# Layer 0's up projection: two more plain features, the token sums spread by a table, jobs in a queue, sums fetched ahead

## Chip, cores and metric

The kernel runs on one core of one Trainium2 chip. The metric is the device time of one execution in microseconds (us); the profile shows one execution, instruction by instruction. The engines are TensorE (PE; its weight loads are listed as PEld), VectorE (DVE), ScalarE (ACT), GpSimd (POOL) and SyncE (SP), which issues most transfers.

## The reference, cut to what matters

One sequence of 512 tokens, 1024 channels, two layers. The change lies in layer 0's gated MLP, with 2816 hidden features:

```python
def conv_glu_ffn(h, w_in, conv_w, conv_b, w_out):
    u = h @ w_in                                  # "up": 1024 -> 2 x 2816
    c = causal_depthwise_conv(u, conv_w, width=3) + conv_b
    a, g = c[..., :D_FF], c[..., D_FF:]
    return (a * jax.nn.silu(g)) @ w_out           # "down": 2816 -> 1024

hn = rms_norm(h, norm_ffn[i])
h = h + conv_glu_ffn(hn, ffn_w_in[i], ffn_conv_w[i], ffn_conv_b[i], ffn_w_out[i])
```

## The kernel before, in words

Activations lie with the channels on the 128 partitions and the 512 tokens along the row, in 8 tiles `h`. Every product is made of three matmuls (`mm3`, L85 to L89): weight and activation are split in a high part, which ScalarE rounds (L101, L402, L426), and a low part, the remainder, which VectorE or GpSimd subtracts (L104, L403, L427). The three are high x high, high x low, low x high.

Layer 0's MLP is `mlp_halves` (L359). A hidden *feature* j is 128 value columns and 128 gate columns, 22 in all.

- *Plain features* (`PLAIN` = 5, j = 0 to 4) are two *chunks* each, gate then value (`todo`, L483). A chunk multiplies 8 weight blocks by 512 tokens: 24 matmuls, 512 wide. Its weights (`load`, L487) come by SP into one of three `raw` buffers, and GpSimd does the low part, 256 columns at a time. The chunk runs on the unnormed input; the norm's statistics (`norm.stats`, at half of chunk 2, L508) and their spread over the partitions (`norm.spread`, in chunk 3, L510) come meanwhile, and `late` (L383) multiplies the finished chunk in its bank by `rb`, then convolves it, applies silu to the gate (`gated`) or multiplies by the gate and splits (`valued`, which appends to the list `z`).
- *Features by sums* (j = 5 to 21) halve tokens and channels and make seven products of half the width in place of eight: with sums of token halves (tiles `th`, `tl`, built once for all features by `first_part` and `second_part`, L405 and L415, mostly on VectorE) and sums of weight blocks R, U, W, Q (`half_weights`, L430). U is fetched by SP and completed by a transfer issued from GpSimd that adds on landing (L441); GpSimd then makes W of R and U (L444, L445). A product is 4 blocks of 3 matmuls, 256 wide: 12; a feature has 84. Between products ScalarE copies parts out (`s1`, `s2`, `s3`, tag `sn`) and VectorE puts the result together (L562, L567, L568), then `gated` and `valued` run directly.
- *Down* is a stream of units: `down(g)` (L455) takes a group of features of `z` (`DOWN0` = 3, 5, 5, 5, 4) and goes over the 8 output tiles m; a unit is one `mm3`, 512 wide, 176 in all. Its weights go through the `raw` buffers too, one step (one m) ahead. `fill` (L533) puts units between the products of a feature, 6 per feature for j = 6 to 9, and 10 for j = 10 to 21; 32 units are left after the loop. When the last group has finished tile m, `after0` splits it for the attention and adds its square to the next norm (L210 to L213, tag `sq`, two buffers).

All parts and late chunks come out in one place in the code: in chunk 3, first all four first parts, the first late chunk, all four second parts (L513 to L517), and from then on each pending chunk at the end of a plain chunk. The first `half_weights` stands in the last plain chunk (L506), each further one at the start of the feature before its use.

The engines work off their own queues in order. The builder may bring an independent instruction forward in its queue; `pin` keeps the order of the code. PSUM has 8 banks: `rings` hands them out in turn, 6 to up (`ps`), and 6 and 7 to the norm and down (`aux`); the attention's first product uses 6 and 7 as well.

Of the kernel before, what the change touches and what calls it, by code (L numbers as in the profile page):

```python
# [26 lines left out]
P = 128  # L27
D = 1024
S = 512
# [31 lines left out]
def trunk(ctx: ExitStack, tc: tile.TileContext, x_tok, x_t, vecs, w_pool, w_kq, w_v, w_o, gain, w_in, w_half, w_down, w_end, w_tok, out):  # L61
# [288 lines left out]
    def conv_sum(fp, ps, m, name):  # L350

        cw = [col(V_CW + t * 2 * NF + m) for t in range(3)]
        t = fp.tile([P, S], F32, tag="t", name=f"{name}_t", bufs=4)
        A.activation(t, ps, AF.Identity, bias=col(V_CB + m), scale=cw[2])
        V.scalar_tensor_tensor(t[:, 1:], ps[:, : S - 1], cw[1], t[:, 1:], ALU.mult, ALU.add)  # L355
        V.scalar_tensor_tensor(t[:, 2:], ps[:, : S - 2], cw[0], t[:, 2:], ALU.mult, ALU.add)  # L356
        return t

    def mlp_halves(fp, xs, norm, ws0, after):  # L359

        lo, hi = slice(0, HS), slice(HS, S)
        z, gate = [], {}
        th, tl, ys = [], [], []

        def gated(j, ps):
            gate[j] = conv_sum(fp, ps, NF + j, f"g{j}")
# [2 lines left out]
        def valued(j, ps):  # L369
            t = conv_sum(fp, ps, j, f"a{j}")  # L370
            V.tensor_tensor(t, t, gate.pop(j), ALU.mult)
            own = j % 10 < 2
            zh, zl = (
                fp.tile([P, S], F32R, tag=f"z{k}", name=f"z{j}{k}", bufs=2)
                if own
                else xp.tile([P, S], F32R, tag=f"x{k}", name=f"z{j}{k}")
                for k in "hl"
            )
            A.activation(zh, t, AF.Copy)
            V.tensor_tensor(zl, t, zh.bitcast(F32), ALU.subtract)  # L380
            z.append((zh, zl))
# [5 lines left out]
        def spare(i, name):  # L387
            return fp.tile([P, 1024], F32R, tag="vh" if i % 6 < 3 else "vl", name=name, bufs=3)
# [26 lines left out]
        def second_part(p):  # L415
            y = ys[p]
            v = spare(p + 4, f"tv{p}").bitcast(F32).rearrange("p (a b) -> p a b", a=4)
            V.tensor_tensor(v[:, 0, :], y[:, 3, :], y[:, 2, :], ALU.add)
            V.tensor_tensor(v[:, 1, :], y[:, 3, :], y[:, 0, :], ALU.add)
            V.scalar_tensor_tensor(v[:, 2, :], y[:, 2, :], -1.0, v[:, 1, :], ALU.mult, ALU.subtract)  # L420
            V.tensor_tensor(v[:, 3, :], y[:, 1, :], v[:, 2, :], ALU.subtract)
            split_part(v, p, 3, 7)

        def own_split(raw, name):
            x, y = (fp.tile([P, 1024], F32R, tag=f"v{k}", name=f"{name}_{k}", bufs=3) for k in "hl")
            A.activation(x, raw, AF.Copy)  # L426
            V.tensor_tensor(y, raw, x.bitcast(F32), ALU.subtract)  # L427
            return x, y

        def half_weights(j):  # L430

            src = w_half[j - PLAIN]
            n = 4 * P
            u = fp.tile([P, 1024], F32, tag="ur", name=f"uw{j}_u_raw", bufs=2)
            r = wp.tile([P, 1024], F32, tag="raw", name=f"uw{j}_r_raw", bufs=3)
            q = wp.tile([P, 1024], F32, tag="raw", name=f"uw{j}_q_raw", bufs=3)
            u2, r2 = (t.rearrange("p (a b) -> p a b", a=2) for t in (u, r))
            nc.sync.dma_start(u2, src[:, 0:4:2, :])
            nc.sync.dma_start(r2, src[:, 0:2, :])
            nc.sync.dma_start(q[:, :n], src[:, 3, :])  # L440
            pin(G.dma_start(u2, src[:, 2:4, :], accum_op=ALU.add))  # L441
            R = weights(None, 2 * n, f"uw{j}_r", raw=r)
            U = own_split(u, f"uw{j}_u")
            G.tensor_tensor(r[:, :n], r[:, :n], u[:, n:], ALU.add)  # L444
            G.tensor_tensor(r[:, n:], r[:, n:], r[:, :n], ALU.add)  # L445
            W = own_split(r, f"uw{j}_v")
            Q = weights(None, n, f"uw{j}_q", raw=q)
            return R, U, W, Q
# [6 lines left out]
        def down(g):  # L455

            first, n = sum(DOWN0[:g]), DOWN0[g]
            def load(m):
                w = weights(w_down[g][m], n * P, f"wo{g}_{m}")
                return [part(w, k) for k in range(n)]  # L460

            w = load(0)
            for m in range(NC):
                ps = bank("aux")
                for k in range(n):
                    mm3(ps, w[k], z[first + k], k == 0, k == n - 1)
                    if k == 0 and m + 1 < NC:
                        ahead = load(m + 1)
                    if k == n - 1:
                        V.tensor_tensor(h[m], ps, h[m], ALU.add)  # L470
                        if g == len(DOWN0) - 1:
                            after(m)
                    yield
                w = ahead

        for c in range(NC):
            if c == 0:
                norm.add(c)
                continue
            sq = norm.square(c, 0, S, fp.tile([P, S], F32, tag="t", name=f"n0_sq{c}", bufs=4))  # L480
            V.tensor_tensor(norm.acc, norm.acc, sq, ALU.add)  # L481

        todo = [(j, s) for j in range(PLAIN) for s in (1, 0)]  # L483
        signs = rb = ws = None
        pend, parts = [], []

        def load(i):  # L487
            if i < len(todo):
# [2 lines left out]
        def chunk(i):  # L491
            if i == 6:
                rings["ps"][:0] = [6, 7]
            ps = bank("ps")
            pend.append((*todo[i], ps))
            return ps

        w, pss = [load(i) for i in range(2)], [chunk(i) for i in range(2)]
# [3 lines left out]
        ahead = load(2)  # L502
        for at in range(2, len(todo)):
            w, ps, ahead = ahead, chunk(at), load(at + 1)
            if at == len(todo) - 1:
                ws = half_weights(PLAIN)  # L506
# [12 lines left out]
            if rb is not None:  # L519
                for x in pend:  # L520
                    late(*x)
                pend.clear()

        LAG = (6, 10, 14, 18, NF)
        plan = {}
        for g in range(len(LAG) - 1):
            f0, f1 = LAG[g : g + 2]
            n = NC * DOWN0[g]
            for i, f in enumerate(range(f0, f1)):
                plan[f] = n * (i + 1) // (f1 - f0) - n * i // (f1 - f0)  # L530
        fills = (None for g in range(len(DOWN0)) for x in down(g))

        def fill(j, i):  # L533
            n = plan.get(j, 0)
            for x in range(n * (i + 1) // 4 - n * i // 4):
                next(fills)

        last = None
        for j in range(PLAIN, NF):
            R, U, W, Q = ws  # L540
            if j == LAG[0]:
                rings["ps"] = [i for i in rings["ps"] if i < 6]
            if j + 1 < NF:
                ws = half_weights(j + 1)
            ba, bx = bank("ps"), bank("ps")
            s1, s2, s3 = (fp.tile([P, HS], F32, tag="sn", name=f"sn{j}{i}", bufs=5) for i in range(3))
# [12 lines left out]
            product(bx[:, hi], U, 1, 4)  # L559
            fill(j, 2)  # L560
            product(ba[:, lo], Q, 0, 6, False)
            V.tensor_tensor(ba[:, hi], bx[:, hi], s3, ALU.add)  # L562
            gated(j, ba)

            def last(j=j, bx=bx, W=W, s1=s1, s2=s2):
                product(bx[:, hi], W, 1, 2, False)
                V.tensor_tensor(bx[:, lo], bx[:, lo], s1, ALU.subtract)  # L567
                V.tensor_tensor(bx[:, hi], s2, bx[:, hi], ALU.subtract)  # L568
                valued(j, bx)

            fill(j, 3)
        last()
        for x in fills:
            pass

# [639 lines left out]
```

## Time and profile before

| | before |
|---|---|
| median of 3 runs | 945.26 us (943.94 to 947.0) |
| the profiled execution, its own time | 942.96 us |
| its span, first to last instruction | 941.3 us |
| mean granted TensorE clock | 0.983 |
| PE busy | 902.2 us (96%), 4884 matmuls |
| VectorE busy | 696.5 us (74%) |
| ScalarE busy | 483.9 us (51%) |
| GpSimd busy | 242.8 us (26%) |
| chain that ended last | PE 82%, DVE 7%, ACT 4%, DMA 3% |

The page cuts the span into 40 slices and gives the busy share of each engine in tenths, and the granted clock in tenths of full speed. The view by stage gives busy time in stretches that one chooses. A view of waits names, for one engine, who ended its idle time: total us, times, longest. In the list in order of time a row is start, length, engine, line, operation, output<-inputs, shapes, and in brackets the idle time before it and who ended it.

### The profile page before, as it was taken

The numbers are of one execution on the slowest core, as the hardware profiler recorded it, in microseconds if no ns is written. First come the engines' busy times: TensorE is split into PE (matmuls) and PEld (weight loads), VectorE is DVE, ScalarE is ACT, GpSimd is POOL, SyncE is SP. The second block draws the span as 40 slices with busy tenths as digits, with TensorE's granted clock in tenths as the row PEclk, the third lists the DMA queues.
The fourth block names the chain that finished last, engine by engine and source line by source line (L and its number), as shares of the span: only waits on it lengthen the run. The fifth ranks groups of instructions, "written<-read, shape, count | busy, mean of one in ns | idle before, by whom it ended". The sixth has DMA issues, their size and how long they took to land.

```text
span 941.3 us, 13168 instructions
## 1 busy us (share of the span) xinstructions
PE 902.2 (96%) x4884; PEld 780.2 (83%) x4884; DVE 696.5 (74%) x1110; ACT 483.9 (51%) x778; POOL 242.8 (26%) x309
## 2 busy tenths in 40 slices
PE   9997499999999999999999999999999999999996
PEld 8785498889999999879888888888888888888885
DVE  7895787776776777585587755498896888976744
ACT  7754454544555545364688653375353444434434
POOL 3753313221311311051766422000230001210004
PEclk9999699999999999999999999999999999999998
DMA  8422265546455453142211014216358322443312
GB/s 315 141 85 45 78 169 134 149 135 172 119 152 167 114 151 97 57 146 90 90 46 46 23 45 157 94 61 203 91 125 278 103 99 68 88 136 112 99 36 90
DMA packets 36800, 108.42 MB, mean 115 GB/s; under 512 B 3840, under 2 KB 4864, under 8 KB 36736
## 3 DMA queue, kind: packets, MB, share of 16 engines
q1 hardware_dynamic: 33136, 94.47, 30.2%
q0 software_dynamic: 3600, 13.11, 8.2%
q8 instruction: 38, 0.62, 0.3%
q14 instruction: 26, 0.21, 0.1%
HBM read 105.47 MB, written 2.10 MB: 114 GB/s over the span
## 4 chain that ended last, share of the span: by engine, by line
PE 82%; DVE 7%; ACT 4%; DMA 3%; issue 2%; POOL 2%; DVEq 0%; ACTq 0%; POOLq 0%
PE bank L87 26%; PE bank L88 26%; PE bank L89 26%; DMA uw_u_raw<-w_half 2%; DMA uw_r_raw<-w_half 1%; PE bank L1047 1%; PE bank L1075 1%; POOL wi_l L104 1%; DVE n_acc L481 1%; PE bank L285 1%; PE bank L252 1%; ACT sc L1063 1%; ACT h L329 0%; DVE g_t L355 0%; DVE g_t L356 0%
## 5 line engine op out<-in xcount | busy, mean ns | idle before, releaser
L87 PE MATMUL bank<-f1x_h,wi_h 128*128 128x512 f32 x352 | 137.9, 392 | 0.0
L89 PE MATMUL bank<-f1x_h,wi_l 128*128 128x512 f32 x352 | 137.1, 390 | 0.0
L88 PE MATMUL bank<-f1x_l,wi_h 128*128 128x512 f32 x352 | 137.0, 389 | 0.0
L101 ACT ACTIVATE wi_h<-wi_raw 128x1024 fp32r<-128x1024 f32 x54 | 57.0, 1060 | 86.4 <-PE bank L88 71.3
L444 POOL TENSOR_TENSOR uw_r_raw<-uw_r_raw,uw_u_raw 128x512 f32<-128x512 f32 x17 | 23.0, 1354 | 215.1 <-DVE uw_r_l L104 208.6
L89 PEld LDWEIGHTS bank<-f1x_h,wi_l 128*128 128x128 f32 x352 | 66.1, 188 | 14.0
L87 PEld LDWEIGHTS bank<-f1x_h,wi_h 128*128 128x128 f32 x352 | 66.1, 188 | 13.5
L88 PEld LDWEIGHTS bank<-f1x_l,wi_h 128*128 128x128 f32 x352 | 66.1, 188 | 13.4
L104 DVE TENSOR_TENSOR wi_l<-wi_raw,wi_h 128x1024 fp32r<-128x1024 f32 x44 | 53.8, 1225 | 29.4 <-ACT wi_h L101 28.6
L101 ACT ACTIVATE wo_h<-wo_raw 128x640 fp32r<-128x640 f32 (+3 forms) x48 | 35.1, 736 | 48.1 <-PE bank L88 42.9
L104 POOL TENSOR_TENSOR wi_l<-wi_raw,wi_h 128x256 fp32r<-128x256 f32 x40 | 41.0, 1057 | 30.4 <-ACT wi_h L101 18.7
L87 PE MATMUL bank<-th,uw_r_h 128*128 128x256 f32 x136 | 40.3, 297 | 8.0 <-issue 4.0
L579 DVE TENSOR_TENSOR c_u<-bank,n_rb 128x512 f32<-128x512 f32 x44 | 30.0, 686 | 21.5 <-PE bank L89 21.5
L89 PE MATMUL bank<-th,uw_r_l 128*128 128x256 f32 x136 | 39.5, 292 | 6.0 <-DVE uw_r_l L104 6.0
L87 PE MATMUL bank<-th,uw_v_h 128*128 128x256 f32 x136 | 39.0, 287 | 5.2 <-ACT sn L549 5.2
L213 POOL TENSOR_TENSOR n_acc<-n_acc,n_sq 128x512 f32<-128x512 f32 x14 | 21.5, 1532 | 81.7 <-ACT n_sq L204 81.6
L584 DVE SCALAR_TENSOR_TENSOR c_t<-c_u,vec,c_t 128x510 f32<-128x510 f32 x44 | 40.9, 931 | 1.2
L87 PE MATMUL bank<-th,uw_u_h 128*128 128x256 f32 x136 | 39.2, 288 | 2.4 <-ACT sn L554 2.4
L88 PE MATMUL bank<-tl,uw_r_h 128*128 128x256 f32 x136 | 39.8, 293 | 0.0
L427 DVE TENSOR_TENSOR uw_v_l<-uw_r_raw,uw_v_h 128x1024 fp32r<-128x1024 f32 x17 | 20.8, 1225 | 25.6 <-ACT uw_v_h L426 25.4
L88 PE MATMUL bank<-tl,uw_u_h 128*128 128x256 f32 x136 | 39.5, 290 | 0.0
L89 PE MATMUL bank<-th,uw_u_l 128*128 128x256 f32 x136 | 39.3, 290 | 0.0
(438 smaller groups left out, 2864.1 us busy)
## 6 DMA issues: line engine op xcount, KB each, us to landing
wi_raw<-w_in SPq DMA_DIRECT2D x54, 512.0 KB, 3.3
uw_u_raw<-w_half SPq DMA_DIRECT2D x17, 512.0 KB, 4.6
uw_r_raw<-w_half SPq DMA_DIRECT2D x17, 512.0 KB, 4.5
uw_u_raw<-w_half POOLq DMA_DIRECT2D x17, 512.0 KB, 6.9
wo_raw<-w_down SPq DMA_DIRECT2D x24, 320.0 KB, 3.5
wt_a_raw<-w_tok SPq DMA_DIRECT2D x12, 512.0 KB, 4.4
kq_raw<-w_kq SPq DMA_DIRECT2D x10, 512.0 KB, 3.4
uw_q_raw<-w_half SPq DMA_DIRECT2D x17, 256.0 KB, 3.2
```

The lines of the kernel that those rows point to most:

```text
L87: T.matmul(ps, lhsT=wh, rhs=xh, start=start, stop=False, **kw)
L88: T.matmul(ps, lhsT=wh, rhs=xl, start=False, stop=False, **kw)
L89: T.matmul(ps, lhsT=wl, rhs=xh, start=False, stop=stop, **kw)
L101: pin(A.activation(h[:, :n], raw[:, :n], AF.Copy))
L104: (eng or V).tensor_tensor(l[:, o], raw[:, o], h[:, o].bitcast(F32), ALU.subtract)
L213: eng.tensor_tensor(self.acc[:, lo:hi], self.acc[:, lo:hi], sq[:, lo:hi], ALU.add)
L252: T.matmul(banks[-1][:, :BW], lhsT=warm[:, :P], rhs=warm, start=True, stop=True)
L285: T.matmul(banks[c][:, i * P : i * P + n], lhsT=xt[:, i, c * P : (c + 1) * P], rhs=sband[:, c // 2, :n], start=(i == 0), stop=(i == NT - 1 ...
L427: V.tensor_tensor(y, raw, x.bitcast(F32), ALU.subtract)
L444: G.tensor_tensor(r[:, :n], r[:, :n], u[:, n:], ALU.add)
L579: V.tensor_tensor(u, ps, rb, ALU.mult)
L584: V.scalar_tensor_tensor(t[:, 2:], u[:, : S - 2], cw[0], t[:, 2:], ALU.mult, ALU.add)
```

## The change

- `PLAIN` is 7: features 5 and 6 become plain, 14 chunks in all; sums serve j = 7 to 21.
- Finished chunks and, in the loop, finished gates and values go into a list `jobs`; `work()` runs the oldest. After each plain chunk a table says what is put there: `0` a first part, `2` a second part, `1` a job, `f` a fetch of sums, `r` and `v` the two halves of the weight splits for the first feature by sums, `m` the first down weights. When the loop begins, four jobs are left; each feature calls `work()` three times and adds two jobs.
- The statistics stand at the start of chunk 3 instead of the middle of chunk 2, their spread five blocks later.
- `half_weights` falls into `fetch_sums` (u, its adding transfer, r), now called two features ahead, `first_weights` (q's fetch, splits of R and U, the sums W) and `second_weights` (splits of W and Q), later in the feature.
- Down's groups are 4, 4, 4, 4, 4, 2; `FILL` gives 11, 11, 10, 11, 11, 10 units to features 7 to 12 and 8 to each further one (136), and 40 units are left after the loop. Its weights go into the two `sq` buffers, fetched two steps ahead and split one ahead. Down's banks are two others.
- Buffers: `t` 3 instead of 4, `sn` 4 for two tiles a feature, `s3` in the one `sqa` buffer, own `z` tiles for j < 4 and the last three features (4 buffers instead of 2).

```diff
-DOWN0 = (3, 5, 5, 5, 4)
-PLAIN = 5
+DOWN0 = (4, 4, 4, 4, 4, 2)
+PLAIN = 7
...
-    def half_weights(j):
+    def fetch_sums(j):
             src = w_half[j - PLAIN]
+            u = fp.tile([P, 1024], F32, tag="ur", name=f"uw{j}_u_raw", bufs=2)
+            nc.sync.dma_start(blocks(u), src[:, 0:4:2, :])
+            pin(G.dma_start(blocks(u), src[:, 2:4, :], accum_op=ALU.add))
+            r = wp.tile([P, 1024], F32, tag="raw", name=f"uw{j}_r_raw", bufs=3)
+            nc.sync.dma_start(blocks(r), src[:, 0:2, :])
+            raws[j] = u, r
...
+        def down_fetch(i):
+            if i < len(steps):
+                g, m = steps[i]
+                n = DOWN0[g] * P
+                down_raw[i] = sm.tile([P, S], F32, tag="sq", name=f"wo{g}_{m}_raw")
+                nc.sync.dma_start(down_raw[i][:, :n], w_down[g][m])
...
+            for i, (g, m) in enumerate(steps):
+                n, first = DOWN0[g], sum(DOWN0[:g])
+                ps, w = bank("aux"), down_w.pop(i)
                 for k in range(n):
                     mm3(ps, w[k], z[first + k], k == 0, k == n - 1)
-                    if k == 0 and m + 1 < NC:
-                        ahead = load(m + 1)
+                    if k == 0:
+                        down_split(i + 1)
+                        down_fetch(i + 2)
...
-                if at == 2 and k == NC // 2:
+                if at == 3 and k == 0:
                     r = norm.stats(bank("aux"), root=True)
-                if at == 3 and k == 1:
+                if at == 3 and k == 5:
                     rb = norm.spread(bank("aux"), r)
                     signs = spread_signs()
-                    for p in range(4):
-                        first_part(p)
-                    late(*pend.pop(0))
-                    for p in range(4):
-                        second_part(p)
...
+            for x in {3: "00", 4: "00", 5: "1", 6: "22", 7: "12", 8: "21", 9: "1f1", 10: "1", 11: "1r", 12: "1vf", 13: "1m1"}.get(at, ""):
...
+        FILL = dict(zip(range(PLAIN, NF), (11, 11, 10, 11, 11, 10, 8, 8, 8, 8, 8, 8, 8, 8, 8)))
...
+        ring = rings["ps"]
+        rings["aux"] = ring[2:4]
+        rings["ps"] = ring[:2] + ring[4:]
...
             if last:
                 last()
+            work()
             fill(j, 0)
             product(ba[:, lo], W, 0, 5, False)
             A.activation(s2, ba[:, lo], AF.Copy, scale=-1.0)
+            if j + 1 < NF:
+                second_weights(j + 1)
+            if j + 2 < NF:
+                fetch_sums(j + 2)
             product(bx[:, lo], R, 1, 1)
             fill(j, 1)
+            work()
...
-            gated(j, ba)
+            jobs.append((gated, j, ba))
+            work()
```

More of the change, by code (lines that the diff above doesn't have):

```diff
@@ L453, in product, with down_split, down @@
                 mm3(out, part(w, 4 * b + p), x, start and p == 0, p == 3, skip_group_check=True)
[L455 to L464, printed above, removed]
+        steps = [(g, m) for g in range(len(DOWN0)) for m in range(NC)]
+        down_raw, down_w = {}, {}
+        def down_fetch(i):
[4 more added lines that the diff above has]
+                nc.sync.dma_start(down_raw[i][:, :n], w_down[g][m])
+        def down_split(i):
+            if i < len(steps):
+                g, m = steps[i]
+                w = weights(None, DOWN0[g] * P, f"wo{g}_{m}", raw=down_raw.pop(i))
+                down_w[i] = [part(w, k) for k in range(DOWN0[g])]
+        def down():
+            for i, (g, m) in enumerate(steps):
+                n, first = DOWN0[g], sum(DOWN0[:g])
+                ps, w = bank("aux"), down_w.pop(i)
                 for k in range(n):
                     mm3(ps, w[k], z[first + k], k == 0, k == n - 1)
-                    if k == 0 and m + 1 < NC:
-                        ahead = load(m + 1)
+                    if k == 0:
+                        down_split(i + 1)
+                        down_fetch(i + 2)
                     if k == n - 1:
@@ L473, in down @@
                     yield
-                w = ahead
         for c in range(NC):
@@ L479, in mlp_halves, with work @@
                 continue
-            sq = norm.square(c, 0, S, fp.tile([P, S], F32, tag="t", name=f"n0_sq{c}", bufs=4))
+            sq = norm.square(c, 0, S, fp.tile([P, S], F32, tag="t", name=f"n0_sq{c}", bufs=3))
             V.tensor_tensor(norm.acc, norm.acc, sq, ALU.add)
         todo = [(j, s) for j in range(PLAIN) for s in (1, 0)]
-        signs = rb = ws = None
-        pend, parts = [], []
+        jobs, fetched = [], 0
+        def work(n=1):
+            for x in range(min(n, len(jobs))):
+                f, *args = jobs.pop(0)
+                f(*args)
         def load(i):
@@ L494, in chunk @@
             ps = bank("ps")
-            pend.append((*todo[i], ps))
+            jobs.append((late, *todo[i], ps))
             return ps
@@ L519, in mlp_halves @@
[L519 to L531, printed above, removed]
+                mm3(ps, part(w, k), xs[k], k == 0, k == NC - 1)
@@ new lines, in mlp_halves @@
+            for x in {3: "00", 4: "00", 5: "1", 6: "22", 7: "12", 8: "21", 9: "1f1", 10: "1", 11: "1r", 12: "1vf", 13: "1m1"}.get(at, ""):
+                if x == "0":
+                    first_part(len(th))
+                elif x == "2":
+                    second_part(len(tv))
+                elif x == "1":
+                    work()
+                elif x == "f":
+                    fetch_sums(PLAIN + fetched)
+                    fetched += 1
+                elif x == "r":
+                    first_weights(PLAIN)
+                elif x == "m":
+                    down_fetch(0)
+                    down_fetch(1)
+                    down_split(0)
+                else:
+                    second_weights(PLAIN)
@@ L562, in mlp_halves @@
             V.tensor_tensor(ba[:, hi], bx[:, hi], s3, ALU.add)
-            gated(j, ba)
+            jobs.append((gated, j, ba))
+            work()
             def last(j=j, bx=bx, W=W, s1=s1, s2=s2):
@@ L568, in last @@
                 V.tensor_tensor(bx[:, hi], s2, bx[:, hi], ALU.subtract)
-                valued(j, bx)
+                jobs.append((valued, j, bx))
             fill(j, 3)
         last()
+        work(len(jobs))
         for x in fills:
```

43 lines of the change are left out of this document (20 added, 23 removed).

## The prediction

> **What bounds the kernel now.** I read the slices of the page first, then the busy time by stage, then the matmul queue alone, and last the three other engines where the matmuls stop.
>
> ```profile
> PE   9997499999999999999999999999999999999996
> ...
> PEclk9999699999999999999999999999999999999998
> ```
>
> TensorE (PE) works nearly everywhere; the only deep dip, with the granted clock down beside it, lies in slices 4 and 5, some 94 to 141 us in: the place where layer 0's up goes from plain features to features by sums. The busy times by stage (stretch and its length, then busy us with the count for PE, weight loads, VectorE, ScalarE and GpSimd, then granted clock, DMA share and GB/s) put it more sharply:
>
> ```profile
> 38.00:46.00 8.00, 5.84 (x31) 4.67 (x30) 5.93 (x11) 3.43 (x5) 5.76 (x7) 1.00 0.22 75
> 46.00:86.00 40.00, 39.75 (x179) 32.73 (x178) 30.72 (x46) 17.57 (x21) 21.34 (x20) 1.00 0.29 84
> 86.00:118.00 32.00, 13.44 (x63) 11.61 (x62) 24.57 (x34) 15.97 (x24) 7.69 (x6) 0.67 0.22 58
> 118.00:200.00 82.00, 76.14 (x513) 69.77 (x513) 63.82 (x89) 43.02 (x68) 19.45 (x16) 0.96 0.56 150
> 200.00:396.00 196.00, 196.00 (x1305) 180.57 (x1304) 141.78 (x196) 99.19 (x147) 41.15 (x29) 1.00 0.47 131
> 396.00:420.00 24.00, 21.79 (x93) 16.78 (x92) 19.57 (x25) 16.71 (x25) 9.70 (x13) 1.00 0.46 142
> ```
>
> From 200 to 396 us PE is never idle: there the stage is pure matmul work and nothing but fewer matmuls could shorten it. Before that it is not. To price the loss I need the pace of an undisturbed matmul and the borders of the stage, from the matmuls in order of time (start, length, instruction):
>
> ```profile
> 85.51 0.39 PE L89 MATMUL bank<-f0x_h,wi_l 128*128 128x512 f32 x1
> ...
> 86.19 0.39 PE L89 MATMUL bank<-f0x_h,wi_l 128*128 128x512 f32 x1
> 90.62 0.55 PE L87 MATMUL bank<-th,uw_r_h 128*128 128x256 f32 x1 [4.04 <-issue]
> ```
> ```profile
> 220.93 0.28 PE L87 MATMUL bank<-th,uw_r_h 128*128 128x256 f32 x1
> ...
> 222.00 0.28 PE L87 MATMUL bank<-th,uw_r_h 128*128 128x256 f32 x1
> ```
> ```profile
> 416.78 0.39 PE L87 MATMUL bank<-ax_h,kq_h 128*128 128x512 f32 x1
> ```
>
> Three 512-wide matmuls start 0.68 us apart (85.51 to 86.19), so one is 0.227; nine 256-wide ones take 1.07 (220.93 to 222.00), so one is about 0.12. A plain chunk is 24 wide ones, 5.44 us, a plain feature two of them, 10.9. A feature by sums is 7 products of 12 narrow ones, 84 x 0.12 = 10.1. A down unit is three wide ones, 0.68. From the first product by sums (90.62) to the first matmul of the attention (416.78) pass 326.2 us; the work in it is 17 x 10.1 + 176 x 0.68 = 291.4. So some 35 us are lost there, and 4.2 more between the end of the last plain matmul (86.19 + 0.23) and 90.62. Of these, 86 to 118 holds 32 - 63 x 0.12 = 24.5 us; 118 to 200 holds the idle 5.9 us (82 - 76.1) and (1 - 0.96) x 82 = 3.3 of clock, 9.2; the rest is thin, and some of it at the end. Two smaller waits stand outside these sums or at the seam to the attention:
>
> ```profile
> PE bank L219 <- DVE n_acc L481: 2.2, 1, 2.2
> PE bank L87 <- DVE h L470: 1.1, 2, 0.8
> PE bank L87 <- ACT z21h L379: 1.1, 1, 1.1
> ```
>
> Why PE stops at 86 us is read on the other engines:
>
> ```profile
> 70.08 7.98 POOL L104 TENSOR_TENSOR wi_l<-wi_raw,wi_h 128x256 fp32r<-128x256 f32 x4 [3.74 <-ACT wi_h L101]
> 78.01 1.02 POOL L441 DMA_DIRECT2D uw_u_raw<-w_half  x1
> 103.68 1.52 POOL L444 TENSOR_TENSOR uw_r_raw<-uw_r_raw,uw_u_raw 128x512 f32<-128x512 f32 x1 [24.64 <-DVE uw_r_l L104]
> ```
> ```profile
> 86.06 1.06 ACT L426 ACTIVATE uw_u_h<-uw_u_raw 128x1024 fp32r<-128x1024 f32 x1 [10.78 <-DMA uw_u_raw<-w_half]
> ```
> ```profile
> 87.67 0.69 DVE L380 TENSOR_TENSOR z0l<-a_t,z0h 128x512 fp32r<-128x512 f32 x1 [9.70 <-ACT z0h L379]
> ```
>
> The adding transfer is queued on GpSimd behind the last plain chunk's split, leaves at 78.01 and lands 8 us later. ScalarE stands in front of it for 10.78 us with finished work queued behind (z0h, the convolutions); VectorE then stands 9.70 us for z0h. The eight late chunks come after that, all before the first sums are usable.
>
> **The change part by part.**
>
> *Two more plain features.* They trade 2 x 10.1 us of matmuls for 2 x 10.9: +1.6 us on the path, and they remove two features' sums and their adding transfers (both off the path).
>
> *Root statistics four products later.* PE would reach them about 2.7 us (4 x 0.68) later, past the 2.2 us wait for n_acc: -2.0, leaving 0.2. The square ring loses a buffer (4 to 3); this is hidden by the same 2.7 us, and costs up to 0.5 without them.
>
> *The table: parts and late chunks over plain chunks 3 to 13.* Nothing of VectorE's work goes away; the question is whether it fits.
>
> ```profile
> 50.00:110.00 60.00, 43.83 (x193) 35.97 (x192) 48.71 (x71) 29.16 (x39) 22.02 (x17) 0.86 0.18 50
> ```
>
> From 50 to 110 us VectorE did 48.7 us: all eight parts, all but one late chunk and one feature's splits, contention with GpSimd included. That is nearly the new table's content (ten late chunks, eight parts, the splits of the first sums). In the new kernel the plain matmuls end near 86.4 - 2.0 + 4 x 5.44 = 106 us, so about 56 us are there for about 50: it fits, at 90%. Then the first feature by sums finds its operands and the first adding transfer, queued four chunks (21.8 us) ahead of its use, landed. I take 1 us of the 24.5 as staying, with 0 to 10 as bounds (the upper: ScalarE's 10.78 us wait repeated once). Next in line after that stall is PE itself. Gain 23.5.
>
> *Jobs, four of them left over at the loop.* The two chunks each of features 5 and 6 come into the loop and go three jobs per feature instead of two, so they are gone after four features.
>
> ```profile
> L384 DVE TENSOR_TENSOR bank<-bank,n_rb 128x512 f32<-128x512 f32 x9 | 6.0, 688 | 1.2 <-ACT n_rb L233 1.2
> ...
> L355 DVE SCALAR_TENSOR_TENSOR g_t<-bank,vec,g_t 128x511 f32<-128x511 f32 x5 | 3.7, 741 | 0.0
> ```
>
> A gate job costs VectorE 0.69 + 2 x 0.74 = 2.2 us, a value job two further products of about 0.69, 3.6. Between 200 and 396 VectorE spent 141.78 us on 196 / 16.9 = 11.6 features (one is 10.1 + 10 units x 0.68), 12.2 each. Features 7 to 10 now last 10.1 + 11 x 0.68 = 17.6 and ask for 12.2, one extra job of 2.9 and about 0.7 of a down step more (1.4 us, add and split): 16.5, 94%. Features 13 on last 15.5 and ask for 12: 77%. So PE stays the bound, narrowly at first.
>
> *Sums fetched two features ahead, down weights in the square ring.* SP's queue gains order, not transfers: u and r go out a feature earlier, past the down fetches, which go two units ahead in two buffers of their own and no longer take the three `raw` buffers from r and q. GpSimd's adding transfer is queued behind the running feature's two sums and in front of the next one's; GpSimd waits in it, and ScalarE's split of u with all behind it (the sn copies that PE needs) would wait if it lands late:
>
> ```profile
> uw_u_raw<-w_half POOLq DMA_DIRECT2D x17, 512.0 KB, 6.9
> wo_raw<-w_down SPq DMA_DIRECT2D x24, 320.0 KB, 3.5
> ```
>
> 6.9 us against half a feature of 7 to 8 and then the whole of the next before PE needs the product: it fits. Of the 9.2 us lost at 118 to 200 I leave 1, bounds 0 to 8. Gain 8.2. The single buffer for s3, one `t` and one `sn` less cost nothing while PE leads by a whole product; without that lead at most one product each, 12 x 0.12 = 1.4.
>
> *Down by 4, 4, 4, 4, 4, 2.* The matmuls are the same 176 units. 40 units instead of 32 are left for after the loop, the first 24 without need of z21, so the 1.1 us wait for it goes, and the down banks are no longer those of the attention's first product, so its 0.8 goes: -1.9. But the last eight steps are now two units long, 1.36 us, and their weights share two buffers with the squares of the norm:
>
> ```profile
> 402.11 0.62 ACT L204 ACTIVATE n_sq<-h 128x512 f32<-128x512 f32 x1
> 403.15 0.63 ACT L101 ACTIVATE wo_h<-wo_raw 128x512 fp32r<-128x512 f32 x1 [0.42 <-PE bank L88]
> ```
> ```profile
> 403.38 0.69 DVE L470 TENSOR_TENSOR h<-bank,h 128x512 f32<-128x512 f32 x1
> 403.99 1.07 DVE L104 TENSOR_TENSOR wo_l<-wo_raw,wo_h 128x512 fp32r<-128x512 f32 x1
> 404.98 0.74 DVE L241 SCALAR_TENSOR_TENSOR ax_l<-h,vec,ax_h 128x512 fp32r<-128x512 f32 x1
> ```
> ```profile
> 410.93 1.79 POOL L213 TENSOR_TENSOR n_acc<-n_acc,n_sq 128x512 f32<-128x512 f32 x1 [1.43 <-ACT n_sq L204]
> ```
>
> Per step VectorE owes 0.69 + 0.74 and a split of 256 columns (not in the trace; between 0.3, about half of the shortest of these rows, and the 1.07 of 512): 1.8 to 2.5 against 1.36. And a buffer is held by weights for a transfer (at most 3.5), two splits (at most 1.7), by a square for 0.62 + 1.79: 5 to 7.6 us of two buffers a step, 2.5 to 3.8 a step, on five or six steps. Excess (2.5 - 1.36) x 5 = 6 up to (3.8 - 1.36) x 6 = 14, and down to 2 where the weights get the buffers first and the squares wait. I take 6.
>
> *The sum*, against the profiled execution's own 942.96 us: +1.6 - 2.0 - 23.5 - 8.2 - 1.9 + 6.0 = -28.0, so 915.0. The median of the runs shown, 945.26, is 2.3 above it; I forecast 917 for a median.
>
> The Trainium skill (TensorE: Matmul & The Clock Gate, Part 1: The HAM clock gate) says that PE drops to half its clock after an idle window of about 3.4 us and needs a busy one to return, so that shorter gaps would cost only themselves. Here 86 to 118 agrees (0.67), but the 0.96 of 118 to 200, where no wait of such length stands in the matmul queue, speaks for a clock that falls earlier; by that the tail's 6 us could cost one more window of half clock, an estimate of 1.7 us.
>
> **The rivals.**
>
> *A: the stall shrinks but stays (faster by 8 to 17 us).* One adding transfer still comes too late: it is held on GpSimd behind the split of plain chunk 13 as it was behind chunk 9. ScalarE then waits up to 10.8 us, as at 86.06, and the clock halves for it: 28 - 10.8 - 3 = 14 gained, 931. For it: the second one is asked for in chunk 12. Against: the first is four chunks ahead. Two extra bad terms of another kind (tail at 14, features 7 to 10 behind by 1 us each) give about the same. Chance 0.1.
>
> *B: GpSimd becomes the bound of the plain stage.*
>
> ```profile
> L104 POOL TENSOR_TENSOR wi_l<-wi_raw,wi_h 128x256 fp32r<-128x256 f32 x15 | 12.9, 890 | 8.0 <-ACT wi_h L101 8.0
> ```
>
> That is 46 to 70 us: 0.89 a quarter, 3.6 a chunk. Beside VectorE's sums of the second parts it was 7.98 a chunk (70.08), above the 5.44 of PE. If all eight chunks split from then on went at 7.98, they would take 64 us of the 50 that there are before chunk 13's start, and the end comes 14 us later: gain 14, 931. Against: the slow quarters come only beside the second parts, four of some nineteen table entries. Chance 0.06. The Trainium skill (SBUF — State Buffer, section Who interferes with whom) has the rule behind it: a VectorE instruction with two SBUF inputs locks out a GpSimd one that reads SBUF for its whole length. By that rule spreading the parts spreads the blocking too; the trace agrees in kind, 0.89 against 2.0 a quarter.
>
> *C: the sums stay where they were and nothing is felt (same).* The order in which the queues really run is made by the builder, which may put the parts back together; then VectorE's 49 us again end after PE's plain end, the 24.5 us come back and the tail eats the rest. Chance 0.04, 943 to 948.
>
> *D: slower.* The last eight steps run strictly one round trip each: square, sum, transfer, two splits, 0.62 + 1.79 + 3.5 + 0.63 + 1.07 = 7.6 us. Six steps then lose 6 x (7.6 - 1.36) = 37 in place of my 6, and the sum becomes +3.4, 949 against the median. It decides from 7.5 us a step. Against: two buffers, not one, and a transfer of 128 KB, below the 320 KB behind the 3.5. Chance 0.03.
>
> **How the numbers follow.** Forecast 0.77, A 0.1, B 0.06, C 0.04, D 0.03. Within the forecast the unknown costs reach from all stalls gone (28 + 1 + 1 + 6 + 3 of the thin rest = 39 below, 906) to two of them near their ends (917 + 12 = 929). I take 904 to 930. A measurement of this kernel tells about 0.3% (2.8 us) from no change; faster by more holds the forecast, A and B: 0.93, same 0.04, slower 0.03.
>
> **What would show it.** Right: PE busy without a gap over 1 us from 46 us to the end of the loop; clock 1.0 between 86 and 200; the statistics' wait for n_acc gone; ScalarE without a wait over 3 us on an adding transfer; plain matmuls ending near 106; waits of PE on wo_l, wo_h or h only in the last steps, 2 to 14 us in all. Wrong: waits on wi_l in the plain stage (B), a ScalarE wait of 5 to 11 us on u (A), or a first product by sums that starts 5 us and more after the last plain matmul.

## The result, and the profile after

| | before | after |
|---|---|---|
| median of 5 runs each, on one chip | 944.77 us (943.87 to 947.0) | 939.86 us (938.07 to 940.62) |
| ratio of the times, 95% interval | | 0.9941 (0.9923 to 0.9959) |
| the profiled execution, its own time and span | 942.96, 941.3 us | 939.86, 938.2 us |
| matmuls, mean granted clock | 4884, 0.983 | 4812, 0.981 |

Faster, but by 4.9 us and not by 28: the forecast of 917 and its range (904 to 930) missed the time. The slices of the page after, in the two rows that were shown of before, tell it at once: the dip is shallower and one slice further right, and a new, shallow one lies in slices 17 and 18.

```profile
PE   8999679999999999879999999999999999999996
...
PEclk9999869999999999989999999999999999999999
```

The busy times by stage, for the same stretches and with the same columns as in the prediction:

```profile
38.00:46.00 8.00, 7.82 (x39) 6.29 (x38) 6.04 (x10) 4.34 (x7) 6.90 (x9) 1.00 0.40 127
46.00:86.00 40.00, 39.61 (x177) 32.49 (x176) 37.83 (x51) 20.14 (x26) 24.85 (x26) 1.00 0.38 107
86.00:118.00 32.00, 22.64 (x103) 18.24 (x101) 21.63 (x29) 14.36 (x20) 12.28 (x11) 0.89 0.34 90
118.00:200.00 82.00, 75.67 (x477) 68.58 (x477) 63.98 (x90) 42.18 (x65) 15.69 (x12) 0.92 0.48 132
200.00:396.00 196.00, 193.76 (x1276) 177.58 (x1275) 151.37 (x211) 101.95 (x155) 43.06 (x31) 1.00 0.46 126
396.00:420.00 24.00, 16.90 (x48) 10.80 (x49) 13.72 (x19) 11.14 (x18) 14.88 (x33) 0.79 0.24 82
```

The first stretch is full now (7.82 of 8 against 5.84), but 396 to 420 holds 48 matmuls where it held 93. For every matmul I take the time from the start of the one before it, less the pace of that one (0.227 us wide, 0.12 for all others), and count it where the matmul starts. That gives what PE lost, by the same sum for both kernels; it is good to about half a microsecond a row:

| us lost by PE | before | after | change | forecast |
|---|---|---|---|---|
| statistics (30 to 90) | 3.1 | 1.5 | -1.6 | -2.0 |
| the seam (90 to 120, after: 90 to 140) | 25.3 | 20.2 | -5.1 | -23.5 |
| from there to 200 | 10.0 | 0.7 | -9.3 | -8.2 |
| 200 to 370 | 1.4 | 1.2 | -0.2 | 0 |
| end of down, start of the attention (370 to 430) | 3.4 | 15.5 | +12.1 | +4.1 |
| two more plain features | | | | +1.6 |

With the 1.6, which is worked out and not measured, that is -2.5, against -3.1 between the spans; 0.6 is not placed. Two rows went as forecast, and two did not: the seam and the end. What PE waits for (who, total us, times, longest, from 46 to 445 us):

```profile
PE bank L87 <- ACT wo_h L101: 12.4, 4, 8.4
PE bank L87 <- ACT sn L577: 4.2, 1, 4.2
PE bank L89 <- DVE wo_l L104: 3.5, 4, 2.1
PE bank L89 <- DVE kq_l L104: 3.2, 1, 3.2
PE bank L89 <- POOL wi_l L104: 1.0, 1, 1.0
```

Of the waits quoted of before, those for h and z21h are gone, and the one for n_acc fell from 2.2 us to 0.2. **At the seam** PE stops four times, in order of time:

```profile
102.05 0.50 PE L89 MATMUL bank<-f0x_h,wi_l 128*128 128x512 f32 x1 [1.01 <-POOL wi_l L104]
117.11 0.80 PE L87 MATMUL bank<-z0h,wo_h 128*128 128x512 f32 x1 [8.35 <-ACT wo_h L101]
120.44 0.80 PE L89 MATMUL bank<-z0h,wo_l 128*128 128x512 f32 x1 [2.11 <-DVE wo_l L104]
126.74 0.58 PE L87 MATMUL bank<-th,uw_v_h 128*128 128x256 f32 x1 [4.22 <-ACT sn L577]
```

The three other engines in the same stretch, GpSimd, ScalarE, VectorE:

```profile
101.27 4.24 POOL L104 TENSOR_TENSOR wi_l<-wi_raw,wi_h 128x256 fp32r<-128x256 f32 x4
105.46 0.89 POOL L438 DMA_DIRECT2D uw_u_raw<-w_half  x1
```
```profile
113.77 1.06 ACT L427 ACTIVATE uw_u_h<-uw_u_raw 128x1024 fp32r<-128x1024 f32 x1 [8.20 <-DMA uw_u_raw<-w_half]
```
```profile
115.38 0.69 DVE L104 TENSOR_TENSOR uw_q_l<-uw_q_raw,uw_q_h 128x512 fp32r<-128x512 f32 x1 [7.95 <-ACT uw_q_h L101]
```

It is the picture of before, one feature later. The adding transfer of feature 8, the *second* one, is queued on GpSimd behind the split of the last plain chunk, leaves at 105.46, and ScalarE stands in front of it until 113.77 with the splits of q and of the first down weights (wo_h) queued behind; VectorE stands for q. **At the end** (PE, then ScalarE):

```profile
396.55 0.50 PE L87 MATMUL bank<-z20h,wo_h 128*128 128x512 f32 x1 [2.79 <-ACT wo_h L101]
...
406.01 0.50 PE L87 MATMUL bank<-z20h,wo_h 128*128 128x512 f32 x1 [1.10 <-ACT wo_h L101]
...
412.99 0.80 PE L89 MATMUL bank<-ax_h,kq_l 128*128 128x512 f32 x1 [3.22 <-DVE kq_l L104]
```
```profile
399.10 0.42 ACT L101 ACTIVATE wo_h<-wo_raw 128x256 fp32r<-128x256 f32 x1 [0.63 <-DMA wo_raw<-w_down]
...
405.54 0.42 ACT L101 ACTIVATE wo_h<-wo_raw 128x256 fp32r<-128x256 f32 x1 [1.15 <-DMA wo_raw<-w_down]
```

Weights of the short last steps come late, and then the low part of the attention's first weights (kq_l). Beside the two longest of these waits, 2.79 and 3.22 us, the clock falls to half: 0.79 on average over the stretch.

### The profile page after: what moved, and what is told of

It is laid out like the page before. It is cut to its first block, busy times and chain, and to the rows that moved or that the text cites. A ratio compares the mean times of both kernels' runs of the same rounds, so it can differ in the third digit from the quotient of the medians.

```text
span 938.2 us, 13044 instructions
## 1 busy us (share of the span) xinstructions
PE 902.0 (96%) x4812; PEld 774.6 (83%) x4812; DVE 702.8 (75%) x1116; ACT 482.4 (51%) x776; POOL 248.8 (27%) x319
## 4 chain that ended last, share of the span: by engine, by line
PE 84%; DVE 5%; ACT 4%; POOL 2%; issue 2%; DMA 2%; DVEq 0%; ACTq 0%; POOLq 0%
PE bank L87 27%; PE bank L89 27%; PE bank L88 26%; DMA uw_u_raw<-w_half 2%; POOL wi_l L104 2%; PE bank L1083 1%; PE bank L1111 1%; DVE n_acc L502 1%; PE bank L285 1%; ACT sc L1099 0%; ACT wi_h L101 0%; ACT px_h L240 0%; ACT h L329 0%; DMA xt<-x_tok 0%; PE bank L726 0%
## 5 line engine op out<-in xcount | busy, mean ns | idle before, releaser
L101 ACT ACTIVATE wi_h<-wi_raw 128x1024 fp32r<-128x1024 f32 x58 | 61.3, 1060 | 88.7 <-PE bank L88 72.6
L101 ACT ACTIVATE wo_h<-wo_raw 128x512 fp32r<-128x512 f32 (+2 forms) x56 | 36.9, 660 | 57.5 <-PE bank L88 55.7
L104 POOL TENSOR_TENSOR wi_l<-wi_raw,wi_h 128x256 fp32r<-128x256 f32 x56 | 55.0, 1014 | 34.3 <-ACT wi_h L101 34.3
L89 PE MATMUL bank<-f0x_h,wi_l 128*128 128x512 f32 x112 | 43.7, 390 | 1.0 <-POOL wi_l L104 1.0
L88 PE MATMUL bank<-f0x_l,wi_h 128*128 128x512 f32 x112 | 43.6, 389 | 0.0
L87 PE MATMUL bank<-f0x_h,wi_h 128*128 128x512 f32 x112 | 43.2, 391 | 0.0
L492 DVE TENSOR_TENSOR h<-bank,h 128x512 f32<-128x512 f32 x48 | 32.9, 685 | 12.8 <-PE bank L89 12.5
L104 DVE TENSOR_TENSOR wo_l<-wo_raw,wo_h 128x512 fp32r<-128x512 f32 (+2 forms) x52 | 36.6, 704 | 4.0 <-ACT wo_h L101 2.6
L87 PE MATMUL bank<-th,uw_v_h 128*128 128x256 f32 x120 | 34.6, 288 | 4.2 <-ACT sn L577 4.2
L757 POOL TENSOR_TENSOR wt_a_raw<-wt_a_raw,wt_s_raw 128x1024 f32<-128x1024 f32 x4 | 11.3, 2836 | 101.6 <-DVE wt_a_l L104 101.6
L428 DVE TENSOR_TENSOR uw_v_l<-uw_r_raw,uw_v_h 128x1024 fp32r<-128x1024 f32 x15 | 18.5, 1232 | 25.3 <-ACT uw_v_h L427 25.3
```

The source lines that it names most:

```text
L87: T.matmul(ps, lhsT=wh, rhs=xh, start=start, stop=False, **kw)
L88: T.matmul(ps, lhsT=wh, rhs=xl, start=False, stop=False, **kw)
L89: T.matmul(ps, lhsT=wl, rhs=xh, start=False, stop=stop, **kw)
L101: pin(A.activation(h[:, :n], raw[:, :n], AF.Copy))
L104: (eng or V).tensor_tensor(l[:, o], raw[:, o], h[:, o].bitcast(F32), ALU.subtract)
L757: G.tensor_tensor(r[:, :n], r[:, :n], raws["s1", s][:, :n], ALU.add)
```

## The experiments

The theories. **1:** the seam's loss is the second adding transfer. **2** (its rival): VectorE is late by itself, and reaches PE through ScalarE's queue whatever the transfer does. **3:** the end's loss comes from squares and down weights sharing the two `sq` buffers. **4:** the end is lost because the last steps are too short. **5:** what repaired 118 to 200 is the new place of the down weights. **6** came after the first four runs: VectorE is late because GpSimd's subtractions beside it make its instructions longer. Line numbers behind L437 shift by some lines from kernel to kernel.

### The second adding transfer moved (e1_early_u)

The fetch of u and its adding transfer become a function of their own, `fetch_u`, and those of feature 8 go out right behind those of feature 7, in chunk 9.

```diff
+        us = {}
...
+            u = us.pop(j, None) or fetch_u(j)
...
+                    if fetched == 1:
+                        us[PLAIN + 1] = fetch_u(PLAIN + 1)
```

> The changed kernel with one transfer moved: u of feature 8 (fetch and adding transfer) is issued right behind u of feature 7, in chunk 9 instead of chunk 12; r of feature 8 stays in chunk 12. Theory 1 (the stall at the seam is one late adding transfer, queued on GpSimd behind the split of plain chunk 13 and blocking ScalarE for 8.2 us): that wait is gone, PE's 8.4 us gap at 117 and the half clock behind it too; of some 20 us lost between 100 and 130 at most 3 stay, so 939.9 - 17 = 923, and under 926. Theory 2 (VectorE's backlog is the bound at the seam, the transfer only shows in front of it): ScalarE waits less but PE still waits for wo and sn; at most 8 us gained, 932 to 938.

Measured: 931.33 us (930.61 to 932.57), ratio to before 0.986 (0.984 to 0.988): 8.5 us under the changed kernel. The waits of PE:

```profile
PE bank L87 <- ACT wo_h L101: 4.6, 4, 2.8
PE bank L87 <- ACT sn L586: 4.2, 1, 4.2
PE bank L89 <- DVE wo_l L104: 3.5, 4, 2.3
```

The wait of 8.35 is gone; those for wo_l and sn stay as they were, and the seam still loses 11.7 of 20.2. Theory 1 has two fifths of it, and something else the rest.

### Squares out of the shared buffers (e2_squares_own), and both (e3_both)

The seven squares of the attention's norm that come in down's last group go into the `t` buffers, which are free by then. e3_both has this and the edit above.

```diff
-                            after(m)
+                            after(m, fp.tile([P, S], F32, tag="t", name=f"n1_sqt{m}", bufs=3) if m else None)
```

> The changed kernel with the squares of the attention's norm in the three t buffers, so that down's weights have the two sq buffers to themselves. Theory 3 (the last eight short steps lose time because squares and weights hold each other's buffers): PE's waits on wo_h and wo_l from 396 us on go, the excess of 390 to 420 (15 us with the half clock) falls to 4, 939.9 - 11 = 929. Theory 4 (two-unit steps are shorter than VectorE's and ScalarE's work for one, about 1.9 and 1.8 us against 1.36): PE still waits each step, at most 4 us gained, 936 or more.

> Both edits together. Theories 1 and 3: they lie in different stages and add up, 939.9 - 17 - 11 = 912, between 908 and 918. If the seam or the tail only hands its wait to the next thing in line (theories 2 and 4): 926 or more.

Measured: 931.22 us (929.39 to 932.26), ratio 0.9855 (0.9834 to 0.9877); and 924.27 us (924.09 to 924.54), ratio 0.9783 (0.9762 to 0.9804). The end loses 6.7 instead of 15.5: theory 3 has most of it. The gains nearly add up (8.5 + 8.6 = 17.1 against 15.6), but e3 misses its own forecast for the same reason as e1. What e2 leaves at the end:

```profile
PE bank L89 <- DVE kq_l L104: 3.7, 2, 1.9
```

### The same move in the kernel before (e4_before_early_u)

No part of the change; only the fetches and adding transfers of the first two features by sums go out in plain chunk 6.

```diff
+            if at == 6:
+                us.update({j: fetch_u(j) for j in (PLAIN, PLAIN + 1)})
```

> The kernel before with only its first two adding transfers (features 5 and 6) issued in chunk 6 instead of behind the last plain chunk. Theory 1 in its strong form (the late transfer was the stall before, too): the 24.5 us lost between 86 and 118 fall to under 8, 944.8 - 18 = 927. Theory 2 for the kernel before (VectorE has 49 us of work from 50 us on, and PE's plain stage ends at 86): only the 9.7 us of VectorE's idle time come back, 944.8 - 10 = 935, and the rest of the stall stays, now as waits on the late chunks.

Measured: 935.55 us (934.13 to 938.02), ratio 0.9906 (0.9882 to 0.993). So a few lines in the kernel before gain 9.1 us, more than the whole change. PE then waits for the first sums' splits:

```profile
PE bank L87 <- ACT sn L559: 6.3, 3, 2.7
PE bank L89 <- DVE uw_r_l L104: 6.3, 1, 6.3
```

VectorE is busy here without a break from 51 to 97 us. Both waits come from VectorE's own lateness, hidden in the trace of before behind the late transfer: the stall there had two causes in parallel, and the profile named the one that came last.

### Down weights back in the `raw` buffers (e6_raw_ring)

e1 with one line changed: the fetches of the sums stay two features ahead, but down's weights take turns in the three `raw` buffers again; the squares are alone in `sq`.

```diff
-                down_raw[i] = sm.tile([P, S], F32, tag="sq", name=f"wo{g}_{m}_raw")
+                down_raw[i] = wp.tile([P, 1024], F32, tag="raw", name=f"wo{g}_{m}_raw", bufs=3)
```

> u of feature 8 early, and down's weights back in the three raw buffers beside r and q (still fetched two steps ahead); the squares then have sq alone. Theory 5 (the waits of the kernel before between 118 and 200 us came from r waiting for a raw buffer): they come back, 5 to 9 us between 120 and 200, and against the run with both first edits (924.3) this is 929 to 933. Rival (fetching two features ahead was enough): within 2 us of 924.3.

Measured: 926.82 us (925.46 to 927.21), ratio 0.9815 (0.98 to 0.9829), faster than e1 by 4.5, and 2.6 slower than e3, whose squares do not share with the weights either: between the two forecasts. Busy PE at 118 to 200:

```profile
118.00:200.00 82.00, 80.38 (x513) 73.23 (x514) 61.83 (x84) 39.59 (x63) 19.50 (x15) 0.96 0.47 131
```

Of the losses behind the seam (140 to 370) it brings back 3.3 us (5.1 against 1.8), while the end falls to 6.7 as in e2. So theory 5 has about a third of the 9.3 us. The rest stays repaired without the new place; that fetching two features ahead did it is likely, but no run has that edit alone. Shared with the squares, the new place costs more at the end than it brings here.

### Eight plain features (e7_plain8)

e3 with `PLAIN` = 8, the table stretched over two more chunks, nine units in each later feature.

```diff
-PLAIN = 7
+PLAIN = 8
...
-            for x in {3: "00", 4: "00", 5: "1", 6: "22", 7: "12", 8: "21", 9: "1f1", 10: "1", 11: "1r", 12: "1vf", 13: "1m1"}.get(at, ""):
+            for x in {3: "00", 4: "00", 5: "1", 6: "22", 7: "12", 8: "21", 9: "1", 10: "1", 11: "1f1", 12: "1", 13: "1r", 14: "vf", 15: "1m11"}.get(at, ""):
```

> Both first edits, and one feature more made plain (8), with the table stretched by two chunks: +0.8 us of matmuls, and two chunks (10.9 us) more in which VectorE has only two late chunks (5.8 us) more to do. Theory 2 for what is left at the seam (11 us: VectorE's backlog): some 5 us of backlog go, with the half clock behind them 6 to 9, so 924.3 + 0.8 - 7 = 918. If what is left is only the order of ScalarE's queue at the start of the loop: nothing gained, 925.

Measured: 927.84 us (925.14 to 928.87), ratio 0.9824 (0.9806 to 0.9841), no better than e3. The seam still loses 9.3 against 12.7, through the same wait, and 200 to 370 loses 3.4 against 1.2:

```profile
PE bank L87 <- ACT sn L586: 4.5, 1, 4.5
```

Eleven more us of plain matmuls do not let VectorE catch up. A likely reason, not shown by itself, is that they bring splits on GpSimd and late chunks with them.

### GpSimd's subtractions left out (e8_no_low), or replaced by writes (e12_low_written)

Both are e3. e8 leaves out the low part of the weights of plain chunks 6 to 13, and GpSimd's subtractions with it (the high part stands in for it in the matmuls). e12 leaves out the same part, but GpSimd writes zeros four times in its place.

```diff
+                if i >= 6:
...
+                    for a in range(0, D, 256):
+                        for x in range(4):
+                            G.memset(ll[:, a : a + 256].bitcast(F32), 0.0)
+                    return hh, ll
```

> Both first edits, and the low part of the weights left out in plain chunks 6 to 13 (the third matmul takes the high part again): the same matmuls and the same list for VectorE, but GpSimd has nothing to subtract beside it. Theory 6 (VectorE's backlog at the seam is the 9 us by which GpSimd's reads stretch its instructions from 50 to 107): VectorE's rows of two SBUF inputs fall back to their shortest, 1.22 to 0.69 and 1.76 to 1.21, and of the 11 us lost at the seam at most 3 stay: 924.3 - 9 = 915. Rival (the backlog is the plain amount of work): within 3 us of 924.

> The kernel of the run with both edits (924.3 us), in which GpSimd, in the place of each subtraction for the low part of plain chunks 6 to 13, writes the same quarter four times with zeros: about the same time on its queue by the 2.02 us that a zeroing of 128x2304 takes (4 x 0.22 = 0.9 against 0.89), but nothing is read. It leaves out the low part of these weights, as the run without the subtractions did (910.5 us). Theory 6 as it stands (VectorE loses time because GpSimd READS beside it): VectorE's lengthening at the seam is 0 to 1 us instead of 9, and the time lies within 2 us of 910.5. Rival (any GpSimd access beside it does it, as the 1.99 us of a sum beside the zeroing of vh suggests): the lengthening stays at 5 us or more and the time is 918 to 925. A second rival (the gain of leaving the subtractions out came from GpSimd's free queue, not from VectorE's pace): VectorE at full pace and yet 918 or more.

Measured, one run each: 910.5 and 917.44 us (the kernel before took 943.86 beside e8, and 941.52 beside e12). Groups on VectorE between 49 and 107 us of the changed kernel, of e8, and (49 to 108) of e12; the mean time of one is the second number behind the bar:

```profile
L403 DVE TENSOR_TENSOR tl<-tv,th 128x1024 fp32r<-128x1024 f32 x4 | 5.9, 1490 | 0.0
...
L412 DVE SCALAR_TENSOR_TENSOR ty<-h,vec,px 128x512 f32<-128x512 f32 x4 | 4.4, 1101 | 0.0
L371 DVE TENSOR_TENSOR a_t<-a_t,g_t 128x512 f32<-128x512 f32 x4 | 4.1, 1029 | 0.0
...
L380 DVE TENSOR_TENSOR z0l<-a_t,z0h 128x512 fp32r<-128x512 f32 x1 | 1.2, 1223 | 0.0
```
```profile
L403 DVE TENSOR_TENSOR tl<-tv,th 128x1024 fp32r<-128x1024 f32 x4 | 4.8, 1222 | 0.0
...
L371 DVE TENSOR_TENSOR a_t<-a_t,g_t 128x512 f32<-128x512 f32 x5 | 3.4, 679 | 0.0
L412 DVE SCALAR_TENSOR_TENSOR ty<-h,vec,px 128x512 f32<-128x512 f32 x4 | 3.0, 744 | 0.0
...
L380 DVE TENSOR_TENSOR z0l<-a_t,z0h 128x512 fp32r<-128x512 f32 x1 | 0.7, 691 | 0.1
```
```profile
L403 DVE TENSOR_TENSOR tl<-tv,th 128x1024 fp32r<-128x1024 f32 x4 | 4.8, 1218 | 0.0
L229 DVE TENSOR_SCALAR n_d<-ident,n_r 128x128 f32<-128x128 f32 x4 | 4.5, 2138 | 0.0
...
L371 DVE TENSOR_TENSOR a_t<-a_t,g_t 128x512 f32<-128x512 f32 x5 | 3.4, 680 | 0.0
```

All four groups of the changed kernel read two operands from SBUF, and all are longer than in e8, by a fifth to three quarters. Over all of VectorE's instructions that start in that stretch (each against the shortest of its line and form) this is 9.2 us in the changed kernel, 9.6 in e3, 0.5 in e8 and 0.3 in e12; the long scalings of e12 (L229), of which below, start before it. In e8 the seam's loss falls from e3's 12.7 to 1.2, as theory 6 says. But e8 also empties GpSimd's queue, and that is what e12 is for. The busy times from 50 to 107 us, of the changed kernel and of e12 (VectorE is the third and GpSimd the fifth number behind the length):

```profile
50.00:107.00 57.00, 55.99 (x247) 45.99 (x247) 53.44 (x71) 30.79 (x40) 34.21 (x32) 1.00 0.31 90
```
```profile
50.00:107.00 57.00, 56.03 (x244) 46.38 (x245) 49.83 (x80) 34.29 (x45) 34.50 (x120) 0.97 0.39 117
```

GpSimd is as busy in e12 (34.50 against 34.21 us), only without reading, and VectorE has done 80 instructions in less time than 71 before: GpSimd's *reads* lengthen VectorE's instructions. Its forecast of 910.5 missed by 7 all the same, for a reason of its own, in the waits of PE from 46 to 150 us:

```profile
PE bank L230 <- DVE n_d L229: 2.9, 1, 2.9
PE bank L87 <- ACT sn L595: 2.0, 1, 2.0
```

The spread's four scalings (L229, else 0.28 us each) were held up by the zeroing and took 4.5 us; the wait of 2.9 and the half clock after it cost 4.8, and VectorE, that much later, left 2.4 at the seam instead of 1.2. With GpSimd as busy as ever, the seam thus loses 2.4 instead of 12.7: VectorE's pace is enough for most of it. One thing e12 does not hold fixed: zeros need no rounded weights, so PE's wait for wi_l, 1.5 us in e3, is gone in it as in e8. That this and a freer GpSimd queue are a small part of the gain is not excluded.

### The short group first (e9_short_first), and with shared buffers (e11_short_first_shared)

`DOWN0` = 2, 4, 4, 4, 4, 4 in place of 4, 4, 4, 4, 4, 2: in e9 on top of e3, in e11 on top of e1, with the squares in the shared buffers.

```diff
-DOWN0 = (4, 4, 4, 4, 4, 2)
+DOWN0 = (2, 4, 4, 4, 4, 4)
```

> Both first edits, and down's short group first instead of last: groups 2, 4, 4, 4, 4, 4, the same 176 units and the same 40 after the loop, the last eight steps of four units, 2.72 us. Theory 4 for the rest of the tail (7 us: VectorE's and ScalarE's work for a step against 1.36 us): 4 to 6 us gained, 919. Rival (the rest is the attention's weights meeting GpSimd's memsets and sums): at most 1.5 us.

> u of feature 8 early and the short group first, but the squares back in the two sq buffers beside down's weights. Theory 4 (the last steps are too short; sharing only bites with them): within 2 us of the run with own squares, 917 to 919. Theory 3 (sharing by itself): the tail's 7 to 9 us come back, 924 or more.

Measured: e9 916.83 us (916.44 to 918.18), ratio 0.9714 (0.9698 to 0.973), the fastest of all; e11 922.69 us (921.72 to 923.12), ratio 0.9767 (0.9741 to 0.9793). In e9 the end is whole:

```profile
390.00:420.00 30.00, 30.00 (x181) 26.79 (x181) 20.77 (x42) 12.37 (x18) 12.31 (x30) 1.00 0.33 105
```

The end loses 14.6 in e1, 6.7 in e3 (own squares), 4.3 in e11 (long steps, shared buffers) and nothing in e9 (both). So theories 3 and 4 are both true, and neither edit alone is enough.

### ScalarE's order pinned (e10_pinned)

e9, with ScalarE's instructions of `late`, `gated`, `valued` and the copies of parts kept in the order of the code, so that the copy PE waits for is not behind other work.

```diff
-            A.activation(s1, ba[:, lo], AF.Copy)
+            pin(A.activation(s1, ba[:, lo], AF.Copy))
```

> The run with the short group first (916.8), and the ScalarE instructions of jobs and the three sn copies held in the order of the code, so that the copy s1 of feature 7 stands ahead of the four leftover jobs instead of behind two of them. Theory 7 (GpSimd's reads make VectorE late, but PE waits for it only because s1 is queued behind work that waits for VectorE): the 4.6 us wait on sn and the half clock behind it go, 916.8 - 6 = 911. Rival (VectorE's lateness reaches PE whatever the order): the wait moves to wo_l or to a down bank, 915 or more.

Measured: 920.47 us (919.95 to 921.01), ratio 0.9747 (0.9726 to 0.9768): slower than e9 by 3.6.

```profile
PE bank L87 <- ACT sn L586: 3.1, 2, 2.9
PE bank L87 <- ACT sn L592: 1.3, 1, 1.3
PE bank L87 <- ACT wo_h L101: 0.9, 2, 0.6
```

The wait for sn shrinks from 4.6 to 2.9, and the seam from 12.3 to 9.2, but 4.9 us come back between 140 and 370, and 0.7 before 90. That places 2.5 of the 2.8 us between the spans of the two profiled executions. It fits a lateness that is VectorE's, where the order on ScalarE only chooses where it is felt.

## Why the prediction was wrong, step by step

*Right.* The statistics (-1.6 against -2.0), the losses up to 200 (-9.3 against -8.2, of which e6 takes back 3.3 with the place of the weights alone), the jobs in the loop (140 to 200, mostly features 8 to 10, loses 0.7, so the 94% held there), the waits for z21h and for the down banks.

*The step that failed* is "it fits, at 90%. Then the first feature by sums finds its operands and the first adding transfer, queued four chunks (21.8 us) ahead of its use, landed. I take 1 us of the 24.5 as staying". 20.2 stayed, for two reasons, both with rows in the trace of before.

First, the term looked at the first adding transfer alone, which kept ScalarE for only 2.33 us and PE not at all. The second one (the second `f` of the table, in chunk 12) went into GpSimd's queue behind the split of chunk 13, exactly the mechanism of rival A. That rival had a chance of 0.1 because one row, "the first is four chunks ahead", was put against it; the question to ask was which is the *last* transfer that ScalarE meets before PE needs something behind it. Its price, a wait of up to 10.8 us, was measured at 8.20 and is worth 8.5 (e1).

Second, the 50 us of VectorE. The 48.7 us counted for before were measured with GpSimd reading beside it for 22 us of the 60; in the plain stage GpSimd splits a whole chunk every 5.44 us, and in the changed kernel it was busy for 34.2 us of 57. The parts, spread over the chunks, met it almost everywhere. VectorE was busy for 53.4 of these 57 us, 9.2 of them pure lengthening (4.6 of the 48.7 in the kernel before, counted in the same way), and was not done at the end. The profile had shown it: the splits of the plain weights at 2.0 us a quarter beside the second parts, against 0.89 alone, were read in rival B as GpSimd's loss. They were a sign of a shared way on which both sides lose, and the side without slack was VectorE. The Trainium skill (SBUF — State Buffer, Who interferes with whom) says that a VectorE instruction with two SBUF inputs contends with a GpSimd instruction that reads SBUF, not with one that only writes, and that it depends on who came first which of the two waits. The runs agree on the first point (9.2 against 0.3 us); on the second they show only that both sides lose (a quarter 2.0 us on GpSimd instead of 0.89, z0l's split 1.22 on VectorE instead of 0.69). The prediction took from it only the direction in which GpSimd waits.

*The end* was mis-sized: +6 with bounds of 2 and 14. The loss grew by 12.1 although the waits priced at 1.9 did go, so the term itself came to 14.0, its upper bound. The buffer held by a weight, then by a square, was the right mechanism (e2: 8.6), the steps too short for their round trip the other (e9, e11). Two things were missing in the sum. One is the clock, which the prediction priced at 1.7 us but did not add: two stretches of half clock, 3.41 and 6.83 us long, lie in the end, so that the waits cost more than their length. The other is the wait of 3.22 us for kq_l, which comes from neither mechanism but from GpSimd (see the last section).

*The counting of parallel causes.* The prediction took the whole stall of 24.5 us off when it had shown one cause, the transfer, and argued the other away. In e4, where only the transfers are moved, 9.1 come; the two largest waits that are left there come from VectorE.

The best version, e9, lands on 917 with three more edits; that is no support for the forecast, since 12.3 us are still lost at its seam.

## What to carry to other kernels

When a stall is to be removed, ask for each engine behind it what it would have been late for on its own: the profile names the last releaser only, and a second cause of nearly the same length lies hidden in its shadow. A budget of busy time taken from one schedule holds for another only if the neighbours are the same, so compare the mean time of one instruction alone and beside the other engine before adding up. A buffer ring shared between a prefetch and a late consumer, and steps shorter than their own round trip, belong at the start of a stream and not at its end.

## What the runs showed of the hardware

- VectorE's TENSOR_TENSOR and SCALAR_TENSOR_TENSOR with two SBUF operands lengthen beside GpSimd reads (z0l's split 0.69 to 1.22 us, the split of tl 1.22 to 1.49 on average) and not beside GpSimd writes (the split of tl 1.22 in e12).
- A VectorE TENSOR_SCALAR behaves the other way: beside GpSimd's zeroing it stood still. In the kernel with the zeros one took 4072 ns where the median is 280 (shortest, median, longest):

```profile
L229 DVE TENSOR_SCALAR n_d<-ident,n_r x12: 269/280/4072, 46.8 to 581.0; 128x128 f32<-128x128 f32 x12
```

In the changed kernel the same is seen at the start of the attention. The VectorE row nsink ends at 412.91, the zeroing of vh on GpSimd at 412.88 (in e9, where nsink ran before that zeroing, it took 0.16 us). kq_l, for which PE waits 3.22 us, is queued behind it. The larger part of that wait is older, though: VectorE stood 2.45 us for another result of GpSimd (qs), which the row in front needs:

```profile
410.83 0.17 DVE L923 TENSOR_TENSOR bqs<-vec,qs 128x8 f32<-128x8 f32 x1 [2.45 <-POOL qs L921]
410.92 1.99 DVE L933 TENSOR_SCALAR nsink<-vec 128x16 f32<-128x16 f32 x1
410.99 2.35 DVE L104 TENSOR_TENSOR kq_l<-kq_raw,kq_h 128x1024 fp32r<-128x1024 f32 x2
```
```profile
410.86 2.02 POOL L929 MEMSET vh<- 128x2304 f32 x1
```

- The clock fell to half beside every wait of PE above 2.2 us that the traces of this case hold behind the first 30 us (2.79 us in the changed kernel, 396.55; 2.88 in e12, 50.97). Between 1.9 and 2.2 us it went either way: it fell after waits of 1.92 (e8, 383.89) and 2.00 us (before, 192.16), and not after 2.04 (e12, 115.04) and 2.16 us (before, 42.89). It stayed down, by the trace's clock record, for 3.4, 6.8 or up to 20.5 us: multiples of 3.4, but for the last one at the end of each execution. The Trainium skill (TensorE: Matmul & The Clock Gate, Part 1: The HAM clock gate) has such a free-running window of 3.4 us; that the stretches are multiples of it agrees, and that a wait shorter than it is enough is what the runs add.
